# Forming the low halves of split weights with an accumulating transfer, in a conformer block

## The chip, the cores and the metric

The kernel runs on one core of one Trainium2 chip. A time is the device time of one execution in microseconds (us). The engines of the core are TensorE (PE, matrix products), VectorE (DVE), ScalarE (ACT), GpSimd (POOL) and SyncE (SP); each works through its own list of instructions in order, and they meet only at semaphores. SP issues nearly all transfers between DRAM and on-chip memory; here a few will be issued by POOL.

## The reference

The block takes a sequence of 1024 tokens with 1024 channels, in float32:

```
h = rms_norm(x, norm1_g)
z = h @ w_in                       # 1024 x (2*1024 + 3*1024 + 2*1024) columns
glu, q, k, v, gates = split(z)
a = value(glu) * sigmoid(gate(glu))          # the gated unit
a = silu(rms_norm(causal_conv31(a)));  y_a = a @ w_conv_out
q, k = rms_norm per head of 64;  o = dilated attention over three groups, 16 heads
y_b = o @ w_attn_out
x = x + (g_a * y_a + g_b * y_b) @ w_out
x = x + gated feed-forward with a convolution of width 3 (2816 wide)
```

Only the projection of `h` onto the columns of the gated unit and of q, k and v is touched by the change.

## The kernel before

**Split products.** A float32 product is made of three faster ones. Each operand is split into a high half, the value rounded to the shorter format (float32r) that TensorE takes, and a low half, the rest. The product is high x high + high x low + low x high. The function `split` (L74) does it: ACT copies the source into the high half (L76), DVE subtracts the high half from the source (L77).

**Weights.** A piece of weights is 128 x 1024 floats, 512 KB. `stage` (L79) has SP load it into a `raw` buffer, and `wsplit` (L84) makes `hi` and `lo` from it. There are four buffers each for `raw`, `hi` (tag `whi`) and `lo` (tag `wlo`), and all weights of the phase use them in turn. A new piece can be split only after the matmuls that read the piece four before it.

**The first phase.** `x` is normalised and transposed into `hT`, split too. Then come:

- the gated unit: for each of 8 channel blocks `c`, a product with a gate piece `g{c}` and one with a value piece `v{c}` (`gemm_ch`, 48 matmuls each), a sigmoid (ACT, L234) and a multiplication (DVE, L237) into `apad`;
- q, k, v: six chunks `ch` (q, k, v, twice), each with four pieces `qkv{ch}_0` to `qkv{ch}_3`. `gemm_tok` (L118) makes one block of 128 tokens by 24 matmuls: for each of 8 steps `k`, high x high (L125), high x low of the weights (L126), low x high (L127); piece `j` serves the steps 2j and 2j+1. Eight token blocks make a chunk, in four PSUM banks. `qkv_head` squares (ACT, L276), sums (DVE, L277), has POOL raise to the power -0.5 (L101) and scales (DVE, L280); `qkv_tail` transposes the result (PE, L288), splits it and stores it in DRAM. The tail lags two token blocks behind;
- the gates (`gate_steps`), and the depthwise convolution of width 31 (`conv_branch`), which is all on DVE: 8 blocks of 31 passes over 128 x 1024 floats (L250, L253).

After that the heads of the attention start (`head`, `score`), in memory that the first phase gives back when the convolution is through.

**The order.** The kernel is written in one order, and a planner sets the order on each engine: it simulates the whole program with its own durations and gives each engine, at each moment, the first written instruction that is ready in the simulation. So DVE works on the convolution, written after q, k, v, in the gaps of the gated unit and of q, k, v. The matmuls of two token blocks can also be interleaved where a piece is late in the simulation. On the chip the order is fixed; every engine waits in place.

Of the kernel before, what the change touches and what calls it, by code (L numbers as in the profile page):

```python
# [12 lines left out]
F32 = mybir.dt.float32  # L13
F32R = mybir.dt.float32r
AF = mybir.ActivationFunctionType
ALU = mybir.AluOpType
# [4 lines left out]
P = 128  # L21
# [29 lines left out]
def block_kernel(ctx: ExitStack, tc: tile.TileContext, x, g1, g2, pack, mask,  # L51
                 w_ch, w_qkv, w_co, w_ao, w_o, w_up, w_down, out):
    nc = tc.nc
    act, dve, pool, pe, sp = nc.scalar, nc.vector, nc.gpsimd, nc.tensor, nc.sync

    cst = ctx.enter_context(tc.tile_pool(name="cst", bufs=1))
    wp = ctx.enter_context(tc.tile_pool(name="wp", bufs=1))
# [4 lines left out]
    def big_ps(name):  # L62
        return psA.tile([P, T], F32, tag="A", name=name)

    def bank_ps(name):
        return psB.tile([P, 512], F32, tag="B", name=name)
# [12 lines left out]
    def stage(src, name):  # L79
        raw = wp.tile([P, 1024], F32, tag="raw", bufs=4, name=f"raw_{name}")  # L80
        sp.dma_start(raw.rearrange("p (a b) -> p a b", a=src.shape[1]) if len(src.shape) == 3 else raw, src)
        return raw

    def wsplit(src, name):  # L84
        hi = wp.tile([P, 1024], F32R, tag="whi", bufs=4, name=f"hi_{name}")[:, : src.shape[1]]
        lo = wp.tile([P, 1024], F32R, tag="wlo", bufs=4, name=f"lo_{name}")[:, : src.shape[1]]
        split(hi, lo, src)
        return hi, lo

    def wpiece(src, name):  # L90
        raw = stage(src, name)
        hi, lo = wsplit(raw, name)
        if len(src.shape) == 3:
            hi = hi.rearrange("p (a b) -> p a b", a=src.shape[1])
            lo = lo.rearrange("p (a b) -> p a b", a=src.shape[1])
        return hi, lo

    def rstd_of(dst, ssq, n, tmp):
# [4 lines left out]
    def gemm_half(o, w, actT, half):  # L103

        hi, lo = w
        ah, al = actT[0][half], actT[1][half]
        for k in range(KT):
            pe.matmul(o, hi[:, k, :], ah[:, k, :], start=(k == 0), stop=False)  # L108
            pe.matmul(o, hi[:, k, :], al[:, k, :], start=False, stop=False)  # L109
            pe.matmul(o, lo[:, k, :], ah[:, k, :], start=False, stop=(k == KT - 1))  # L110
            yield

    def gemm_ch(ps, w, actT):
        for half in range(2):
            for _ in gemm_half(ps[:, half * 512 : half * 512 + 512], w, actT, half):
                pass

    def gemm_tok(ps, actT, wpieces, tt):  # L118

        half, c0 = tt // 4, (tt % 4) * P  # L120
        for k in range(KT):
            hi, lo = wpieces[k // 2]
            ah = actT[0][half][:, k, c0 : c0 + P]
            al = actT[1][half][:, k, c0 : c0 + P]
            pe.matmul(ps, ah, hi[:, k % 2, :], start=(k == 0), stop=False)  # L125
            pe.matmul(ps, ah, lo[:, k % 2, :], start=False, stop=False)  # L126
            pe.matmul(ps, al, hi[:, k % 2, :], start=False, stop=(k == KT - 1))  # L127
# [50 lines left out]
    def hb_tiles(pl, name):  # L178
        t = [[pl.tile([P, KT, 512], F32R, tag=f"hb{a}{h}", name=f"{name}{a}{h}") for a in range(2)]
             for h in range(2)]  # L180
        return [[t[h][a] for h in range(2)] for a in range(2)]
# [15 lines left out]
    with tc.tile_pool(name="ph1", bufs=1) as p1:  # L197
# [4 lines left out]
        for tt in range(8):  # L202
            xx = p1.tile([P, CW - 1 + T], F32, tag="apad", bufs=10, name=f"x_{tt}")[:, 0:T]
            sp.dma_start(xx, x[tt * P : (tt + 1) * P, :])
            xt.append(xx)
            if tt == 3:
                wfirst = [wpiece(w_ch[8], "g0"), wpiece(w_ch[0], "v0")]
# [7 lines left out]
        hT = hb_tiles(hb1, "hT")  # L215
# [12 lines left out]
        for c in range(8):  # L228
            a = p1.tile([P, CW - 1 + T], F32, tag="apad", bufs=10, name=f"apad_{c}")
            pool.memset(a[:, : CW - 1], 0.0)  # L230
            gp = big_ps(f"glug_{c}")
            gemm_ch(gp, wfirst[0] if c == 0 else wpiece(w_ch[8 + c], f"g{c}"), hT)
            sg = t4(f"sg_{c}")
            act.activation(sg, gp, AF.Sigmoid)  # L234
            vp = big_ps(f"gluv_{c}")
            gemm_ch(vp, wfirst[1] if c == 0 else wpiece(w_ch[c], f"v{c}"), hT)
            dve.tensor_tensor(out=a[:, CW - 1 :], in0=vp, in1=sg, op=ALU.mult)  # L237
            apad.append(a)

# [25 lines left out]
        def qkv_head(ch, tt, ps):  # L265
            kind, g8 = ch % 3, ch // 3
            psv = ps.rearrange("p (h d) -> p h d", h=8)
            if kind == 2:
                vt = t4(f"v_{ch}_{tt}", F32R).rearrange("p (h s d) -> p h s d", h=8, s=2)
                split(vt[:, :, 0, :], vt[:, :, 1, :], psv)  # L270
                spill(dv[g8][:, :, tt, :], vt.rearrange("p h s d -> p h (s d)"))
                return None
            sq = p1.tile([P, 512], F32, tag="sq", bufs=2, name=f"sq_{ch}_{tt}")
            ss = p1.tile([P, 8], F32, tag="ss8", bufs=2, name=f"ss8_{ch}_{tt}")
            rs = p1.tile([P, 8], F32, tag="rs8", bufs=2, name=f"rs8_{ch}_{tt}")
            act.activation(sq, ps, AF.Square)  # L276
            dve.tensor_reduce(out=ss, in_=sq.rearrange("p (h d) -> p h d", h=8), axis=AX.X, op=ALU.add)  # L277
            rstd_of(rs, ss, DH, ss)
            qn = p1.tile([P, 512], F32, tag="qn", bufs=3, name=f"qn_{ch}_{tt}")
            dve.tensor_tensor(out=qn.rearrange("p (h d) -> p h d", h=8), in0=psv,  # L280
                              in1=rs.unsqueeze(2).to_broadcast([P, 8, DH]), op=ALU.mult)
            return ch, tt, qn

        def qkv_tail(ch, tt, qn):
            kind, g8 = ch % 3, ch // 3
            pt = big_ps(f"qt_{ch}_{tt}")[:, 0:512]
            for j in range(4):
                pe.transpose(pt[:, j * P : (j + 1) * P], qn[:, j * P : (j + 1) * P], ident)  # L288
            qh = p1.tile([P, 512], F32R, tag="qh", bufs=2, name=f"qh_{ch}_{tt}")
            ql = p1.tile([P, 512], F32R, tag="ql", bufs=2, name=f"ql_{ch}_{tt}")  # L290
            if kind == 0:
                act.activation(qh, pt, AF.Copy, scale=qkg)
                dve.scalar_tensor_tensor(out=ql, in0=pt, scalar=qkg, in1=qh.bitcast(F32),
                                         op0=ALU.mult, op1=ALU.subtract)
            else:
                split(qh, ql, pt)
            dst = dq if kind == 0 else dk
            for s, t in ((0, qh), (1, ql)):
                spill(dst[g8][s][:, :, tt * P : (tt + 1) * P], t.rearrange("p (a b) -> p a b", a=4))

        tails = []
        for ch in range(6):
            kind, g8 = ch % 3, ch // 3
            wpieces = [wpiece(w_qkv[kind * 2 + g8, :, 2 * j : 2 * j + 2, :], f"qkv{ch}_{j}") for j in range(4)]
            for tt in range(8):
                ps = bank_ps(f"qkv_{ch}_{tt}")
                gemm_tok(ps, hT, wpieces, tt)
                tails.append(qkv_head(ch, tt, ps))
                if len(tails) > LAG:
                    t = tails.pop(0)  # L310
                    if t is not None:
                        qkv_tail(*t)
# [161 lines left out]
    with tc.tile_pool(name="ph3", bufs=1) as p3:  # L474
# [48 lines left out]
        for j in range(2):  # L523
            wpieces = [wpiece(w_o[j, :, 2 * i : 2 * i + 2, :], f"wo{j}_{i}") for i in range(4)]
# [32 lines left out]
        def up_first(f):  # L557

            v = stage(w_up[f], f"uv{f}")
            vh, vl = wsplit(v, f"uv{f}")  # L560
            xz = big_ps(f"xz_{f}")
            product(xz[:, 0:512], four(vh)[:, 0:4], four(vl)[:, 0:4], *left[0], True)
            product(xz[:, 512:1024], four(vh)[:, 4:8], four(vl)[:, 4:8], *left[1], True)
            return v, xz
# [46 lines left out]
    with tc.tile_pool(name="ph4", bufs=1) as p4:  # L611
# [43 lines left out]
        for f in range(FT):  # L655
            up_rest(f, *ready.pop(0))
            if f + 1 < FT:
                v, xz = ups.pop(0) if ups else up_first(f + 1)
# [6 lines left out]
    with tc.tile_pool(name="ph5", bufs=1) as p5_:  # L665
# [7 lines left out]
        def gload(k, half, fs, dst=None):  # L673
            raw = dst if dst is not None else p5_.tile([P, G * 512], F32, tag="gr", bufs=4, name=f"gr{k}{half}_{fs[0]}")
            for i, f in enumerate(fs):
                sp.dma_start(raw[:, i * 512 : i * 512 + 512], dff[k * HF + f][:, half * 512 : half * 512 + 512])
            return raw[:, : len(fs) * 512]
# [41 lines left out]
        for fs in groups:  # L719
            e = early.pop(0) if early else None  # L720
            g = gload(0, 0, fs, dst=None if e is None else e[:, 0].bitcast(F32))
# [137 lines left out]
```

## Time and profile before

| | us |
|---|---|
| median of 3 runs (1814.44 to 1816.28) | 1815.06 |
| the profiled execution | 1811.43 |
| its span, first to last instruction | 1809.6 |
| PE busy | 1765.8 |
| DVE busy | 1318.8 |
| ACT busy | 771.6 |
| POOL busy | 195.8 |

The mean clock granted to TensorE is 0.991 of full speed. "Busy" is time with an instruction running; matmuls overlap, so a matmul row of 390 ns in the profile stands for one every 0.227 us when they follow each other. Rows of the timeline give the start, the duration, the engine, the line, the operation, what it writes and reads, and in brackets how long its engine sat idle just before it and what ended that. A row of windows gives busy time (and number of instructions) per engine, the granted clock, the busy share of the DMA engines and the rate.

### The profile page before, as it was taken

To read this page: it belongs to the slowest core of one execution; us is meant where nothing else is said; L and a number is where in the kernel's file an instruction comes from. 1 tells how busy PE (TensorE), PEld (TensorE's weight loads), DVE (VectorE), ACT (ScalarE), POOL (GpSimd) and SP (SyncE) were. 2 spreads that over 40 slices of the span, in tenths; PEclk is the share of its full clock that TensorE was granted. 3 is DMA by queue.
4 is the path that set the end of the run, shared out by engine and by line. 5 is a ranking of instruction groups with operands and counts; after the bars stand their busy time and mean duration, and the time that the engine had idled before them with its cause. 6 is when DMAs were issued, how large, how long until landed. Compare 5 with 4: busy or idle time off the path is not lost.

```text
span 1809.6 us, 22474 instructions
## 1 busy us (share of the span) xinstructions
PE 1765.8 (98%) x8244; PEld 1461.9 (81%) x8244; DVE 1318.8 (73%) x1798; ACT 771.6 (43%) x1202; POOL 195.8 (11%) x197
## 2 busy tenths in 40 slices
PE   7999999999999999999999999989999999999999
PEld 5888888888887888887888878768888888878887
DVE  5999999999735655666654543787777777789863
ACT  4111132232245656666655332545444554543441
POOL 1000133133002122222210000210000000000000
PEclk9999999999999999999999999999999999999999
DMA  5111145345549456666527543313222222389851
GB/s 203 59 47 47 41 134 163 116 134 157 157 173 246 145 158 175 180 165 179 164 70 279 169 160 133 104 48 107 80 82 81 71 95 91 116 303 335 298 180 47
DMA packets 142063, 257.57 MB, mean 142 GB/s; under 512 B 11265, under 2 KB 60545, under 8 KB 141953
## 3 DMA queue, kind: packets, MB, share of 16 engines
q1 hardware_dynamic: 141808, 255.61, 43.8%
q8 instruction: 65, 1.06, 0.3%
q10 hardware_dynamic: 144, 0.52, 0.1%
q14 instruction: 46, 0.37, 0.1%
HBM read 190.03 MB, written 66.06 MB: 142 GB/s over the span
## 4 chain that ended last, share of the span: by engine, by line
PE 53%; DMA 4%; DVE 4%; issue 1%; ACT 1%; SPq 1%; POOLq 0%; POOL 0%; DVEq 0%; ACTq 0%
PE xz L550 5%; PE xz L551 5%; PE xz L552 5%; PE dx L703 5%; PE dy L703 5%; DMA gg<-dya 2%; PE pp L400 2%; PE y L550 2%; PE y L552 2%; PE y L551 2%; PE ya L108 2%; PE ya L109 2%; PE ya L110 2%; PE o L408 2%; PE wo L126 1%; PE wo L127 1%
## 5 line engine op out<-in xcount | busy, mean ns | idle before, releaser
L253 DVE SCALAR_TENSOR_TENSOR cacc<-apad,pk,cacc 128x1024 f32<-128x1024 f32 x240 | 297.7, 1274 | 0.7
L125 PE MATMUL qkv<-hi_qkv,hT 128*128 128x512 f32 x384 | 151.8, 396 | 0.0
L127 PE MATMUL qkv<-hi_qkv,hT 128*128 128x512 f32 x384 | 150.0, 391 | 0.0
L126 PE MATMUL qkv<-lo_qkv,hT 128*128 128x512 f32 x384 | 149.4, 390 | 0.0
L389 DVE CUSTOM_DVE_ANT_0 p<-s,m 128x128 f32<-128x128 f32 (+7 forms) x128 | 95.1, 750 | 62.7 <-PE pp L400 39.0
L77 DVE TENSOR_TENSOR pl<-pp,ph 128x512 fp32r<-128x512 f32 x192 | 103.1, 549 | 49.1 <-ACT ph L76 48.6
L393 POOL TENSOR_SCALAR p<-p,st 128x128 f32<-128x128 f32 (+7 forms) x128 | 94.9, 748 | 335.5 <-DVE st L392 211.9
L76 ACT ACTIVATE ph<-pp 128x512 fp32r<-128x512 f32 x192 | 91.3, 487 | 92.2 <-PE pp L400 89.3
L649 DVE SCALAR_TENSOR_TENSOR u<-u,pk 128x1023 f32<-128x1023 f32 (+1 forms) x88 | 112.3, 1279 | 18.9 <-ACT u L647 18.5
L101 POOL TENSOR_TENSOR rs<-ss,mhalf 128x8 f32<-128x8 f32 (+1 forms) x40 | 80.3, 2010 | 353.1 <-DVE ss L100 353.0
L391 ACT ACTIVATE p<-p,st 128x128 f32<-128x128 f32 (+7 forms) x128 | 99.0, 776 | 14.6 <-DVE st L389 12.9
L108 PE MATMUL gate<-hT,hi_gt 128*128 128x512 f32 x256 | 101.8, 398 | 0.0
L109 PE MATMUL gate<-hT,hi_gt 128*128 128x512 f32 x256 | 100.8, 394 | 0.0
L110 PE MATMUL gate<-hT,lo_gt 128*128 128x512 f32 x256 | 100.3, 393 | 0.0
L400 PE MATMUL pp<-ident,p 128*128 128x128 f32 x576 | 94.4, 277 | 0.0
L127 PEld LDWEIGHTS qkv<-hi_qkv,hT 128*128 128x128 f32 x384 | 72.0, 188 | 15.3
L126 PEld LDWEIGHTS qkv<-lo_qkv,hT 128*128 128x128 f32 x384 | 72.2, 188 | 14.5 <-DVE lo_qkv L77 0.3
L125 PEld LDWEIGHTS qkv<-hi_qkv,hT 128*128 128x128 f32 x384 | 72.2, 188 | 14.0
L400 PEld LDWEIGHTS pp<-ident,p 128*128 128x128 f32 x576 | 69.5, 142 | 10.0 <-issue 0.2
L384 PE MATMUL s<-kh,q 128*128 128x512 f32 (+1 forms) x192 | 69.7, 368 | 7.3 <-DVE st L389 4.8
L408 PE MATMUL o<-ph,v 128*128 128x512 f32 x192 | 73.1, 381 | 3.6 <-ACT ph L76 1.8
L409 PE MATMUL o<-pl,v 128*128 128x512 f32 x192 | 70.5, 369 | 1.6 <-DVE pl L77 1.5
(269 smaller groups left out, 4610.4 us busy)
## 6 DMA issues: line engine op xcount, KB each, us to landing
wr<-w_down SPq DMA_DIRECT2D x45, 512.0 KB, 5.7
gr<-dff SPq DMA_DIRECT2D x62, 256.0 KB, 5.2
raw_qkv<-w_qkv SPq DMA_DIRECT2D x24, 512.0 KB, 3.9
raw_uv<-w_up SPq DMA_DIRECT2D x22, 512.0 KB, 3.3
raw_ug<-w_up SPq DMA_DIRECT2D x22, 512.0 KB, 3.3
dff<-u SPq DMA_DIRECT2D x22, 512.0 KB, 2.6
dv<-v SPq DMA_DIRECT2D x16, 512.0 KB, 3.2
raw_gt<-w_ch SPq DMA_DIRECT2D x16, 512.0 KB, 4.8
```

The lines of the kernel that those rows point to most:

```text
L108: pe.matmul(o, hi[:, k, :], ah[:, k, :], start=(k == 0), stop=False)
L109: pe.matmul(o, hi[:, k, :], al[:, k, :], start=False, stop=False)
L110: pe.matmul(o, lo[:, k, :], ah[:, k, :], start=False, stop=(k == KT - 1))
L125: pe.matmul(ps, ah, hi[:, k % 2, :], start=(k == 0), stop=False)
L126: pe.matmul(ps, ah, lo[:, k % 2, :], start=False, stop=False)
L127: pe.matmul(ps, al, hi[:, k % 2, :], start=False, stop=(k == KT - 1))
L253: dve.scalar_tensor_tensor(out=acc, in0=a[:, j : j + T], scalar=w(j), in1=acc, op0=ALU.mult, op1=ALU.add)
L400: pe.transpose(pp[:, qb * P : (qb + 1) * P], pts[qb][:, kt * P : (kt + 1) * P], ident)
L550: pe.matmul(o, wh[:, k, :], bh[:, k, :], start=(start and k == 0), stop=False, skip_group_check=not start)
L551: pe.matmul(o, wh[:, k, :], bl[:, k, :], start=False, stop=False, skip_group_check=not start)
L552: pe.matmul(o, wl[:, k, :], bh[:, k, :], start=False, stop=(k == 3), skip_group_check=not start)
L703: pe.matmul(banks[n], a[:, c], b[:, d], start=(start and i == 0 and m == 0), stop=(stop and i == nf - 1 and m == 2), skip_group_check=True)
```

## The change

A second way to form a piece, `wpiece_sum`, serves the weights of the gated unit (all but the first two pieces, so 14) and of q, k, v (all 24). The raw piece is still loaded by SP and ACT still copies it into the high half. ACT then writes the negated high half into the `lo` buffer, and a transfer issued by POOL adds the raw weights to it, read a second time from DRAM. DVE's subtraction is gone for these 38 pieces. The other weights (gates and all later phases) keep `wpiece`.

```diff
+    def wpiece_sum(src, name):
+
+        raw = stage(src, name)
+        hi = wp.tile([P, 1024], F32R, tag="whi", bufs=4, name=f"hi_{name}")
+        lo = wp.tile([P, 1024], F32R, tag="wlo", bufs=4, name=f"lo_{name}")
+        act.activation(hi, raw, AF.Copy)
+        act.activation(lo, hi.bitcast(F32), AF.Copy, scale=-1.0)
+        hi = hi.rearrange("p (a b) -> p a b", a=src.shape[1])
+        lo = lo.rearrange("p (a b) -> p a b", a=src.shape[1])
+        pool.dma_start(lo, src, accum_op=ALU.add)
+        return hi, lo
...
-            gemm_ch(gp, wfirst[0] if c == 0 else wpiece(w_ch[8 + c], f"g{c}"), hT)
+            gemm_ch(gp, wfirst[0] if c == 0 else wpiece_sum(w_ch[8 + c], f"g{c}"), hT)
...
-            gemm_ch(vp, wfirst[1] if c == 0 else wpiece(w_ch[c], f"v{c}"), hT)
+            gemm_ch(vp, wfirst[1] if c == 0 else wpiece_sum(w_ch[c], f"v{c}"), hT)
...
-            wpieces = [wpiece(w_qkv[kind * 2 + g8, :, 2 * j : 2 * j + 2, :], f"qkv{ch}_{j}") for j in range(4)]
+            wpieces = [wpiece_sum(w_qkv[kind * 2 + g8, :, 2 * j : 2 * j + 2, :], f"qkv{ch}_{j}") for j in range(4)]
```

## The prediction

> **What bounds the kernel now.** I read the page's busy times first, then the windows of the first phase, then who TensorE waits for. From the page:
>
> ```profile
> PE 1765.8 (98%) x8244; PEld 1461.9 (81%) x8244; DVE 1318.8 (73%) x1798; ACT 771.6 (43%) x1202; POOL 195.8 (11%) x197
> PE   7999999999999999999999999989999999999999
> DVE  5999999999735655666654543787777777789863
> ```
>
> DVE looks full for the first quarter, but so does PE, and the windows say which of them matters (columns: PE, PE weight loads, DVE, ACT, POOL, granted clock, DMA share, GB/s):
>
> ```profile
> 45.00:100.00 55.00, 54.86 (x242) 45.12 (x241) 50.97 (x43) 10.15 (x10) 0.00 (x0) 1.00 0.17 58
> 200.00:250.00 50.00, 50.00 (x234) 41.38 (x233) 48.23 (x57) 14.74 (x20) 14.03 (x7) 1.00 0.22 66
> 400.00:450.00 50.00, 50.00 (x238) 41.33 (x237) 50.00 (x64) 13.25 (x21) 20.24 (x8) 1.00 0.49 146
> 500.00:520.00 20.00, 19.69 (x94) 16.25 (x93) 5.91 (x11) 3.96 (x5) 0.00 (x0) 1.00 0.27 93
> ```
>
> From 45 to 500 us PE is without a gap at full clock, although DVE is at 96 to 100% too. The list of TensorE's waits in the first 420 us confirms it: all of them are in the start-up.
>
> ```profile
> PE tp L190 <- DVE ss L100: 10.7, 2, 9.4
> PE tp L190 <- DVE xs L223: 1.9, 1, 1.9
> PE glug L108 <- ACT hT L76: 0.5, 1, 0.5
> ```
>
> So in this stage PE sets the time and DVE's load is cover: the convolution fills what is left of DVE, and is through just as the gates run. What DVE saves is worth nothing here; what delays a piece of weights is paid in full.
>
> **What is removed from DVE.**
>
> ```profile
> L77 DVE TENSOR_TENSOR lo_qkv<-raw_qkv,hi_qkv x24: 1203/1214/1226, 169.1 to 437.1; 128x1024 fp32r<-128x1024 f32 x24
> L77 DVE TENSOR_TENSOR lo_v<-raw_v,hi_v x8: 1215/1218/1220, 18.1 to 159.8; 128x1024 fp32r<-128x1024 f32 x8
> L76 ACT ACTIVATE hi_qkv<-raw_qkv x24: 1051/1062/1067, 168.0 to 432.6; 128x1024 fp32r<-128x1024 f32 x24
> ```
>
> 24 subtractions of 1.214 us and 14 of 1.218 are 46 us of DVE. They end up as an earlier convolution. Behind it, the nearest places where that could reach PE are the waits as attention opens, below the 500 us mark:
>
> ```profile
> PE s L384 <- DMA kl<-dk: 2.2, 1, 2.2
> 549.60:552.00 2.40, 1.53 (x4) 1.00 (x4) 0.09 (x1) 0.00 (x0) 0.00 (x0) 0.50 0.98 345
> 554.00:556.00 2.00, 1.90 (x6) 1.58 (x6) 1.29 (x8) 2.00 (x8) 0.90 (x3) 0.50 1.05 215
> ```
>
> The first head is loaded into memory that the convolution gives back. An earlier end could remove the 2.2 us, and 6.4 us at half clock behind it (549.6 to 556), worth 3.2. Bounds 0 and -5.4 us; I take -3.
>
> **What is added to ACT and the transfers.** 38 more copies of 1.06 us, 40 us on an engine busy 10 to 15 us of each 50: nothing, as long as no piece is waited for. 38 transfers of 512 KB, 19.9 MB over 450 us, are 44 GB/s on a stage that moves 58 to 146: nothing in sum; in bursts they count, below. `raw` is free after the high copy instead of after DVE, so the loads of raw weights only start earlier.
>
> **The gated unit.**
>
> ```profile
> 102.72 1.06 ACT L76 ACTIVATE hi_g<-raw_g 128x1024 fp32r<-128x1024 f32 x1 [9.82 <-PE glug L109]
> 113.60 1.06 ACT L76 ACTIVATE hi_v<-raw_v 128x1024 fp32r<-128x1024 f32 x1 [8.90 <-PE gluv L109]
> ```
>
> A buffer is freed at the end of a product, every 10.9 us, and its new piece is used three products later: 32.6 us of slack. The longer way of a piece (some 9 us, next part) lies inside it. Cost 0, with 23 us of cover left. The sigmoid queues behind one more ACT copy, 1 us, which nothing but DVE awaits.
>
> **The chunks of q, k, v.** Here the slack is short, since all four buffers hold the chunk in work. The end of chunk 0:
>
> ```profile
> 242.21 1.06 ACT L76 ACTIVATE hi_qkv<-raw_qkv 128x1024 fp32r<-128x1024 f32 x1 [0.76 <-PE qkv L127]
> 243.31 1.23 DVE L77 TENSOR_TENSOR lo_qkv<-raw_qkv,hi_qkv 128x1024 fp32r<-128x1024 f32 x1 [0.16 <-ACT hi_qkv L76]
> 243.57 1.06 ACT L76 ACTIVATE hi_qkv<-raw_qkv 128x1024 fp32r<-128x1024 f32 x1 [0.30 <-PE qkv L127]
> 246.45 0.48 PE L125 MATMUL qkv<-hi_qkv,hT 128*128 128x512 f32 x1
> 246.77 0.40 PE L126 MATMUL qkv<-lo_qkv,hT 128*128 128x512 f32 x1
> ```
>
> The last token block frees piece 0 at 241.9, and piece 1 1.36 us later (6 matmuls of 0.227). PE has 18 matmuls and a group of transposes left, and reads the new low half at 246.77. DVE had it ready at 244.54: 2.2 us to spare. The changed piece goes: high copy at 242.21, two copies of 1.06, done at 244.33. Then POOL issues and the transfer runs. The trace has no accumulating transfer and none issued by POOL, so I bound both. What rows there are, with the median time from issue to landing:
>
> ```profile
> raw_g<-w_ch SPq DMA_DIRECT2D x8, 512.0 KB, 3.3
> raw_qkv<-w_qkv SPq DMA_DIRECT2D x24, 512.0 KB, 3.9
> dq<-qh SPq DMA_DIRECT2D x16, 256.0 KB, 2.5
> x<-x SPq DMA_DIRECT2D x8, 512.0 KB, 8.4
> L81 SPq DMA_DIRECT2D raw_qkv<-w_qkv x24: 327/333/578, 126.9 to 391.7; - x24
> 239.65 2.54 POOL L101 TENSOR_TENSOR rs<-ss,mhalf 128x8 f32<-128x8 f32 x1 [3.10 <-DVE ss L100]
> ```
>
> Transfer: 256 KB more cost 3.3 - 2.5 = 0.8 us. Adding means reading the target too, which is one 512 KB more than the plain load: 3.9 + 1.6 = 5.5 us, nearest to the `raw_qkv` row. Bounds 3.3 (a plain quiet load) and 8.4 (the loads of x, in a queue full of them). Issue on POOL: between 0.33 us (SP's) and 2.54 (POOL's longest instruction here, behind which it may also have to queue); I take 1.0. The low half lands at 244.33 + 1.0 + 5.5 = 250.8, which is 4.1 us after PE wants it. By the low ends 1.2 us late, by the high ends 8.5.
>
> The Trainium skill, "DMA: Bandwidth & Descriptors", section "Specifications", gives first-byte latencies of about 1 us for transfers issued by GpSimd and 0.6 for those of SP. That speaks against the change: by it each landing is 0.4 us later and the sum 2 us larger. No row here shows it.
>
> The other three pieces come behind: ACT makes one per 2.12 us, and each transfer moves twice 512 KB, about 3 us at the 350 GB/s that windows here reach (345 in the row at 549.6). PE, if it interleaves two token blocks, uses a piece for 12 matmuls, 2.7 us. That it does so is shown by two squares close together at the head of the first chunk:
>
> ```profile
> 211.07 0.60 ACT L276 ACTIVATE sq<-qkv 128x512 f32<-128x512 f32 x1 [9.32 <-PE qkv L127]
> 212.20 0.60 ACT L276 ACTIVATE sq<-qkv 128x512 f32<-128x512 f32 x1 [0.53 <-PE qkv L127]
> ```
>
> So they trail by another 0.3 us each, 0.9 in all: 5.0 us of standing PE per transition. There is no other work for PE in that place: the gates need the same four buffers, and the tails bring only transposes. The first chunk is different, since only its fourth piece comes late (copied at 200.69, landing 209.3 by the same sum). Two blocks on three pieces cover 36 matmuls, until 208.9: cost about 0. That leaves 5 transitions, the first with its high copy at 242.21, the last here:
>
> ```profile
> 428.07 1.06 ACT L76 ACTIVATE hi_qkv<-raw_qkv 128x1024 fp32r<-128x1024 f32 x1 [0.76 <-PE qkv L127]
> ```
>
> **The clock behind a stall.** The one long wait of PE in mid-kernel is followed by half clock:
>
> ```profile
> PE y L551 <- DVE blk_t L77: 4.7, 1, 4.7
> PE wo L126 <- DVE lo_wo L77: 1.7, 1, 1.7
> 1180.00:1184.00 4.00, 4.00 (x10) 3.17 (x11) 4.00 (x6) 1.06 (x1) 1.76 (x1) 0.50 0.39 131
> 1060.00:1080.00 20.00, 17.18 (x75) 13.68 (x74) 11.60 (x16) 6.39 (x11) 0.00 (x0) 1.00 0.61 200
> ```
>
> After 4.7 us the clock is 0.50 for 4 us, a loss of 2 us; after 1.7 us it stays at 1.00; after the 2.2 us at `kl` it also fell. A stall of 5 us therefore costs 7. The Trainium skill, "TensorE: Matmul & The Clock Gate", Part 1, has the clock halve after an idle window of about 3.4 us. The trace disagrees at the 2.2 us wait, and the measurement decides. By the page, stalls of 2.2 to 3.4 us would go free of the 2 us, at most 10 us off the sum; with mine, nothing changes.
>
> **POOL's own queue.** Each of the 24 transfers is issued from the list that also holds the powers of L101. A transfer waiting for ACT's copy holds up the power behind it, then DVE's scaling and the transposes of the tail. The tail lags two blocks, 48 matmuls or 10.9 us, and POOL is busy 14 to 20 us of 50; 8 more in 48 us fit. Cost 0, inside the high end above if the cover fails.
>
> **The sum.** Against the profiled execution: 1811.4 + 5 x (5.0 + 2.0) - 3 = 1843.4 us. The median of the runs is 3.6 above that execution, so 1815.06 + 32 = 1847 us.
>
> **The rivals.** (a) *The transfers are slow or queue up.* The four pieces of a transition and the four raw loads for the chunk after it go out within some 10 us. With landings of 8.4 us and 5 us between pieces, the first is 244.33 + 1.0 + 8.4 - 246.77 = 7.0 us late and PE stands 7.0 + 3 x (5 - 2.7) = 14 us, with the clock 16; five of them 80, less 3: 1892 us. For it: the loads of x filled the DMA engines just so (share 1.03); against it: 0.22 to 0.49 in the windows above.
>
> ```profile
> 10.00:20.00 10.00, 6.36 (x31) 4.98 (x29) 9.32 (x14) 9.43 (x18) 1.56 (x6) 0.85 1.03 419
> ```
>
> (b) *The transfers are hidden.* With low ends for issue and landing a piece is 1.2 us late. If the planner puts the high x high matmuls of three more blocks first (0.7 us), PE stands 0.5 us and keeps its clock: 5 x 0.5 - 3, within 1 us of no change, 1814.5 us. Against it: it needs both low ends, and the planner's foresight.
>
> (c) *The early convolution wins.* The place is the opening of attention at 547 us, the price the 5.4 us above. It decides once a transition costs below 0.4 us, that is, with a landing up to 4.0 us after ACT's second copy (2.4 of slack, 0.7 of matmuls put first, 0.4, and some transposes). Then the time is 1815 - 5.4 + 1 = 1811 us. For it: DVE is at 96 to 100% until 489; against it: attention's other waits are for transfers and scores, not for the convolution.
>
> **How the numbers follow.** My forecast 0.62: 1847 us, its own range 1825 (transitions of 2 to 3 us, clock kept) to 1880 (13 each). (a) 0.20, (b) 0.09, (c) 0.09. A change below 0.2%, 3.6 us, can't be told from none here. (c) is faster and a part of (b) falls either way: faster 0.09, same 0.08, slower 0.83. The range goes from 1818, where (b) ends, to 1905, the middle of (a) and something above.
>
> **What would show it.** Right: PE waits at L126 on the landing of `lo_qkv` at five places some 47 us apart, 4 to 6 us each; half clock behind each; no waits in the gated unit; DVE's L77 without `lo_qkv`, and its idle time up in the first 500 us. Wrong: no waits at the chunk heads (b), waits at every piece (a), waits in the gated unit or of the transposes on POOL's powers (a queue that I priced at nothing), or a landing outside 3.3 to 8.4 us.

## The result, and the profile after

The changed kernel takes 1863.08 us (median of 4 runs, 1859.55 to 1864.13) against 1814.75 for the kernel before beside it: a ratio of 1.0268, 95% interval 1.0255 to 1.0281, or 48 us more. Forecast were 32 us more, 1847, with a range of 1818 to 1905. The direction, the place and the clock's part were right; one duration was too short, two parts had been priced at nothing, and one as a gain.

The page after, its busy times and the first slices:

```profile
span 1862.0 us, 22573 instructions
PE 1785.6 (96%) x8244; PEld 1475.3 (79%) x8244; DVE 1277.8 (69%) x1760; ACT 808.2 (43%) x1240; POOL 222.3 (12%) x235
PE   7999988889899999999999999989999999999999
DVE  4999988986124556666564542588777777779963
```

DVE has lost 41 us of work, and the span has grown by 52.4. PE, which had 9s from the second slice on, has 8s from the sixth: q, k, v. The windows that answer to those before (same columns):

```profile
45.00:100.00 55.00, 54.91 (x243) 45.15 (x242) 48.83 (x41) 16.44 (x16) 5.69 (x6) 1.00 0.53 115
200.00:250.00 50.00, 48.43 (x226) 39.89 (x224) 49.05 (x57) 15.69 (x21) 18.23 (x10) 1.00 0.32 79
250.00:300.00 50.00, 44.83 (x199) 36.71 (x200) 43.38 (x54) 11.55 (x19) 17.78 (x10) 0.93 0.54 148
400.00:450.00 50.00, 44.17 (x197) 36.16 (x197) 40.99 (x51) 17.00 (x23) 16.42 (x11) 0.93 0.61 158
```

The gated unit (45 to 200 us) runs as before, PE without a gap: 154.91 us busy of these 155, before 154.86. From 250 us on, 5 to 6 us of each 50 are idle and the granted clock is 0.93. Who TensorE waits for, in the whole run:

```profile
PE qkv L138 <- DMA lo_qkv<-w_qkv: 28.2, 5, 6.1
PE qt L300 <- DVE qn L292: 4.5, 2, 3.5
PE s L396 <- DMA kl<-dk: 1.8, 1, 1.8
```

Five waits on the landing of a low half, 5.6 us each, were not there before, and neither were two on the scaled heads of q and k (`qn`), which PE transposes into `qt`. The transfers themselves (the last figure is the median time to landing, which counts from the start of the issue), their issue on POOL, and the queue that they go through (packets, MB, share of the 16 DMA engines' time):

```profile
lo_qkv<-w_qkv POOLq DMA_DIRECT2D x24, 512.0 KB, 9.4
L107 POOL DMA_DIRECT2D lo_qkv<-w_qkv x24: 865/876/1392, 172.0 to 478.4; - x24
q0 software_dynamic: 5472, 19.93, 6.1%
```

And the head of the second chunk, where the prediction had worked its sum:

```profile
243.04 1.06 ACT L103 ACTIVATE hi_qkv<-raw_qkv 128x1024 fp32r<-128x1024 f32 x1 [0.76 <-PE qkv L139]
244.13 1.06 ACT L104 ACTIVATE lo_qkv<-hi_qkv 128x1024 fp32r<-128x1024 f32 x1
245.50 0.93 POOL L107 DMA_DIRECT2D lo_qkv<-w_qkv  x1 [1.84 <-ACT lo_qkv L104]
247.94 0.48 PE L137 MATMUL qkv<-hi_qkv,hT 128*128 128x512 f32 x1
254.16 0.76 PE L138 MATMUL qkv<-lo_qkv,hT 128*128 128x512 f32 x1 [5.74 <-DMA lo_qkv<-w_qkv]
256.43 0.63 PE L137 MATMUL qkv<-hi_qkv,hT 128*128 128x512 f32 x1
258.53 0.40 PE L139 MATMUL qkv<-hi_qkv,hT 128*128 128x512 f32 x1
```

The copies end at 245.19, POOL issues at 245.50, and PE goes on at 254.16, 8.7 us after the issue. It would have gone on at 248.17, one matmul (0.227 us) after the last one on the high half, so 6.0 us are lost, and the matmuls take 0.63 us instead of 0.40 until 258: half clock. The windows there show where the landing falls. The DMA engines are full:

```profile
248.00:252.00 4.00, 0.43 (x3) 0.11 (x1) 4.00 (x6) 4.00 (x7) 1.65 (x2) 0.96 0.97 196
252.00:256.00 4.00, 1.84 (x4) 1.49 (x5) 4.00 (x6) 1.46 (x2) 3.11 (x3) 0.50 1.04 296
260.00:264.00 4.00, 4.00 (x21) 3.28 (x20) 0.37 (x1) 0.00 (x0) 0.00 (x0) 1.00 1.04 223
```

**Where the 52.4 us of the span come from.** Up to the last matmul of q, k, v it is 47.4 (the last starts at 524.6 instead of 477.2). 28.2 are the waits on landings, 4.5 those on the heads. Six of these seven are followed by half clock, 7 to 13 matmuls at 0.427 instead of 0.227 us, 1.6 to 2.9 us each: 13. The first matmul of q, k, v comes 0.8 later. That is 46.5 of the 47.4. Behind q, k, v are 5 us more. 2.9 of them lie in the product with w_out, where the clock is half for 3.4 us (window clock 0.83) behind a wait that both kernels have; the run with the transfer in the gated unit alone, which is as fast as the kernel before, shows the same 0.83. So I do not put them down to the change. The other 2.1 lie in attention, in small waits.

### The profile page after: what moved, and what is told of

The parts are those of the page before. It is cut to its first block, busy times and chain, and to the rows that moved or that the text cites. A ratio compares the mean times of both kernels' runs of the same rounds, so it can differ in the third digit from the quotient of the medians.

```text
span 1862.0 us, 22573 instructions
## 1 busy us (share of the span) xinstructions
PE 1785.6 (96%) x8244; PEld 1475.3 (79%) x8244; DVE 1277.8 (69%) x1760; ACT 808.2 (43%) x1240; POOL 222.3 (12%) x235
## 4 chain that ended last, share of the span: by engine, by line
PE 52%; DMA 4%; DVE 4%; ACT 1%; issue 1%; SPq 0%; POOL 0%; DVEq 0%; ACTq 0%; POOLq 0%
PE xz L562 5%; PE xz L563 5%; PE xz L564 5%; PE dx L715 5%; PE dy L715 5%; PE pp L412 2%; PE y L562 2%; PE y L563 2%; PE y L564 2%; PE ya L120 2%; PE ya L121 2%; PE ya L122 2%; PE o L420 2%; PE wo L138 2%; PE wo L139 1%; PE wo L137 1%
## 5 line engine op out<-in xcount | busy, mean ns | idle before, releaser
L138 PE MATMUL qkv<-lo_qkv,hT 128*128 128x512 f32 x384 | 155.9, 407 | 28.2 <-DMA lo_qkv<-w_qkv 28.2
L137 PE MATMUL qkv<-hi_qkv,hT 128*128 128x512 f32 x384 | 155.1, 407 | 0.0
L139 PE MATMUL qkv<-hi_qkv,hT 128*128 128x512 f32 x384 | 154.7, 403 | 0.0
L113 POOL TENSOR_TENSOR rs<-ss,mhalf 128x8 f32<-128x8 f32 (+1 forms) x40 | 73.9, 1850 | 132.0 <-DVE ss L112 131.9
L139 PEld LDWEIGHTS qkv<-hi_qkv,hT 128*128 128x128 f32 x384 | 75.6, 197 | 15.9
L137 PEld LDWEIGHTS qkv<-hi_qkv,hT 128*128 128x128 f32 x384 | 75.1, 196 | 15.4
```

## The experiments

Times are medians; "before" is the kernel before, run beside them on the same chip. Each cut of code is against the changed kernel and shortened.

### Which pieces pay

The gated unit alone:

```diff
-wpieces = [wpiece_sum(w_qkv[kind * 2 + g8, ...
+wpieces = [wpiece(w_qkv[kind * 2 + g8, ...
```

> The accumulating transfer serves the gated unit alone; q, k and v keep the subtraction on DVE. Theory (only the chunk heads of q, k, v pay, because all four buffers are in use there and a low half lands some 8.6 us after its issue): within 3 us of the kernel before, no wait of PE on lo_g or lo_v, and none on lo_qkv. Rival 1 (the transfers, POOL's issues or the full DMA engines cost everywhere): 14 of 38 pieces, so about +18 us. Rival 2 (the relief of DVE, 17 us here, is worth something): 3 to 6 us faster than before.

1814.25 us, before 1814.95; ratio 0.9996 (0.9982 to 1.0009). No wait on any low half.

q, k, v alone:

```diff
-gemm_ch(gp, ... wpiece_sum(w_ch[8 + c], f"g{c}"), hT)
+gemm_ch(gp, ... wpiece(w_ch[8 + c], f"g{c}"), hT)
-gemm_ch(vp, ... wpiece_sum(w_ch[c], f"v{c}"), hT)
+gemm_ch(vp, ... wpiece(w_ch[c], f"v{c}"), hT)
```

> The accumulating transfer serves q, k and v alone; the gated unit keeps DVE's subtraction. Theory: as the changed kernel, +45 to +52 us over the kernel before, five waits of PE on lo_qkv of 5 to 6 us each, half clock behind each. Rival 1 (a cost per transfer wherever it is): 24 of 38, so about +31 us.

1858.52 us, 1.0241 (1.0222 to 1.0261): 43.6 us more than before, just under the band that I gave, and well above the 31 of a cost per transfer.

```profile
PE qkv L138 <- DMA lo_qkv<-w_qkv: 31.2, 5, 7.3
```

So the same transfer costs nothing in the gated unit, where 32.6 us of slack cover it, and in q, k, v it costs 43.6 of the 48.3 us, with intervals of the two ratios that overlap.

### What the relief of DVE is worth

```diff
-lo = wp.tile([P, 1024], F32R, tag="wlo", bufs=4, name=f"lo_{name}")
+lo = low0[0]            # written once
 act.activation(hi, raw, AF.Copy)
-act.activation(lo, hi.bitcast(F32), AF.Copy, scale=-1.0)
...
-pool.dma_start(lo, src, accum_op=ALU.add)
```

> The low halves of these 38 pieces are left out: no subtraction, no negated copy, no transfer; all of them read one buffer that is written once. It leaves out part of the computation and measures the relief of DVE (46 us) by itself, with nothing put in its place. Theory (PE sets the time here and the earlier convolution waits for TensorE's fixed order anyway): within 2 us of the kernel before. Rival (an earlier convolution opens attention earlier): 3 to 6 us faster, the wait on kl gone.

1817.97 us, before 1814.95; 1.0011 (0.9999 to 1.0023). With 38 subtractions taken away (46 us by their rows; DVE's busy time falls by 40) and nothing put in their place, nothing is gained. The last pass of the convolution starts at 443.1 instead of 484.8 us, but the first head is loaded no earlier, and its wait stays (first the kernel before, then this run):

```profile
L133 SPq DMA_DIRECT2D kl<-dk x32: 444/594/1199, 541.3 to 878.2; - x32
L143 SPq DMA_DIRECT2D kl<-dk x32: 444/593/1648, 541.2 to 879.7; - x32
PE s L396 <- DMA kl<-dk: 3.5, 1, 3.5
```

In the written order 92 steps of the gates stand between q, k, v and attention, and the multiplication of the convolution's result by its norm starts at 519.2 us here and at 519.3 before. That these steps are the reason is read from the order and was not tried by itself.

### What makes the landing long

The same transfer without the add:

```diff
-pool.dma_start(lo, src, accum_op=ALU.add)
+pool.dma_start(lo, src)
```

> The transfer that POOL issues copies the raw weights over the low buffer and adds nothing, so the low halves are wrong; everything else is as in the changed kernel. Theory (the add itself is dear: it keeps the DMA engines busy about 1.8 times as long as a plain load of the same size, 2.99 against 1.63 us per transfer by the queues' shares): median landing of lo_qkv falls from 9.4 to about 7 us, waits of PE on lo_qkv from 28 to 16 to 20 us, and the time is some 8 to 14 us below the changed kernel. Rival (the cost is POOL's software path, and the add is free): landing 9 us and the time as the changed kernel.

1853.24 us, 9.8 below the changed kernel. The landing falls from 9.4 to 7.0 us, as expected, and the waits from 28.2 to 22.2, less than the 16 to 20 expected:

```profile
lo_qkv<-w_qkv POOLq DMA_DIRECT2D x24, 512.0 KB, 7.0
q0 software_dynamic: 5472, 19.93, 3.4%
L107 POOL DMA_DIRECT2D lo_qkv<-w_qkv x24: 527/537/1027, 172.0 to 470.7; - x24
```

The share of the queue gives the engine time of one transfer: 6.1% of 1862.0 us over 38 is 2.99 us of all 16 engines with the add, 3.4% of 1848.9 over 38 is 1.65 without. The add nearly doubles it (1.8 times) and takes a third of a microsecond more to issue. The Trainium skill, "Collectives: The Full Stack", section "The bandwidth ceiling: the fold count and why AG ≠ RS ≠ AR", has the reducing step of a collective at half the rate of the copying one, because it reads two sources. The transfer here is no collective; its shares come near that, at 1.8.

The adds alone, without the raw loads for the chunks 1 to 5:

```diff
+if ch == 0:
+    raws0 = [stage(w_qkv[0, :, 2 * j : 2 * j + 2, :], f"raw0_{j}") for j in range(4)]
-wpieces = [wpiece_sum(w_qkv[...], f"qkv{ch}_{j}") for j in range(4)]
+wpieces = [wpiece_sum(w_qkv[...], f"qkv{ch}_{j}", raws0[j]) for j in range(4)]
```

> The loads of raw weights for the chunks 1 to 5 of q, k, v are left out: their high halves are made from chunk 0's raw pieces, so they are wrong, and nothing but the accumulating transfers and the spills is moved at a chunk head. Theory (adds and raw loads share DMA engines that are full for some 18 us at each chunk head): the raw loads are 4 x 1.63 of some 22 us of engine time, so the median landing of lo_qkv falls from 9.4 to 6 or 7 us, waits of PE on lo_qkv from 28 to 13 to 20 us, time 8 to 16 us below the changed kernel. Rival (the add's own latency is 8.6 us there and the loads do not matter): landing and time as in the changed kernel.

1844.66 us, 18.4 below the changed kernel, somewhat more than the 8 to 16 expected; landing 6.6 us.

```profile
PE qkv L138 <- DMA lo_qkv<-w_qkv: 19.7, 6, 4.8
lo_qkv<-w_qkv POOLq DMA_DIRECT2D x24, 512.0 KB, 6.6
```

The add with its weights from the chip:

```diff
-pool.dma_start(lo, src, accum_op=ALU.add)
+pool.dma_start(lo, raw.rearrange("p (a b) -> p a b", a=src.shape[1]).bitcast(F32), accum_op=ALU.add)
```

> The accumulating transfer reads the raw weights from their buffer on the chip instead of a second time from DRAM; raw buffers are held until it has landed. Theory (the engine time of the add, 2.99 us per transfer on all 16 engines, and the queue of other transfers at the chunk heads decide, not DRAM): median landing of lo_qkv 8 to 10 us, time within 8 us of the changed kernel. Rival (the second read from DRAM is the slow part): landing 2 us or more shorter and the time 10 us or more below the changed kernel.

1846.69 us, 16.4 below the changed kernel. My figures were missed and the rival's were met, the second read from DRAM as the slow part. But the run changes more than that read. The raw buffer stays in use until the add has landed, so the next chunk's raw loads are issued later. In the changed kernel the first of them is issued at 244.13, ahead of the first add; here it comes behind that add's landing, 4.5 us after the issue:

```profile
245.76 0.92 POOL L107 DMA_DIRECT2D lo_qkv<-raw_qkv  x1 [1.84 <-PE qkv L138]
250.28 0.33 SPq L81 DMA_DIRECT2D raw_qkv<-w_qkv  x1
lo_qkv<-raw_qkv POOLq DMA_DIRECT2D x24, 512.0 KB, 6.1
lo_g<-raw_g POOLq DMA_DIRECT2D x7, 512.0 KB, 4.4
q0 software_dynamic: 5472, 19.93, 5.6%
```

The engine time hardly falls (5.6% of 1845.4 over 38: 2.72 us), but the landing does: by 1.1 us for the gate pieces of the gated unit (5.5 from DRAM), by 3.3 in the median of q, k, v. What PE waits for is the first add of a chunk, and its landings at the five heads separate the parts better than the medians. In the changed kernel they are 7.4 to 8.5 us; without raw loads 5.7 to 7.1, near the 5.5 of the quiet; with the weights from the chip 4.5 to 4.8, near the quiet 4.4. So the larger part, some 2 us, goes with the raw loads, and the second read from DRAM takes 1.1 us in the quiet and 1.2 to 2.3 here; no run takes that read away and leaves the raw loads in their place. The reading that I had set against the rival, a queue of other transfers at the head, is not refuted by this run.

The gain is not all in the landing, either: the waits on landings fall from 28.2 to 11.9 us, and those at the transposes rise from 4.5 to 11.5.

### Whether it is the place: more slack, or fewer late pieces

Two more buffers, and the control with the same cuts and no new buffers:

```diff
-apad bufs=10, t4 bufs=4, sq bufs=2
+apad bufs=9, t4 bufs=2, sq bufs=1          # both runs
...
+hi = own.tile([P, 1024], F32R, tag="xhi", bufs=2, ...)   # piece 0 of a chunk, first run only
+lo = own.tile([P, 1024], F32R, tag="xlo", bufs=2, ...)
```

> The changed kernel with two more buffers: the first piece of each chunk of q, k, v has two of its own, so that the first two pieces of a chunk can be formed while the chunk before is still in work. To make room apad has 9 buffers instead of 10, t4 2 instead of 4, sq 1 instead of 2. Theory (the transfer is fine, its place at the head of a chunk with all buffers in use is the cost): waits of PE on lo_qkv below 8 us in all, time within 15 us of the kernel before, 35 us or more below the run with the same cuts and no new buffers. Rival (DMA time or POOL is the limit): no more than 10 us below that run.

> Control for the run with more buffers: the changed kernel with the same cuts (apad 9, t4 2, sq 1) and no new buffers. Both theories: as the changed kernel, 0 to 10 us more for the cuts.

1831.24 us with the buffers, 1866.62 without: 35 us. The landings are as long as ever, the waits are a third:

```profile
PE qkv L142 <- DMA lo_qkv<-w_qkv: 9.0, 3, 3.9
lo_qkv<-w_qkv POOLq DMA_DIRECT2D x24, 512.0 KB, 9.6
```

The theory's band was missed by a hair (9.0 us of waits where I gave 8, 17.7 us above before where I gave 15); its core, that the same transfers cost less where they have slack, is shown. The 17.7 us that stay are about what the run without any transfer, below, costs; 9.0 of them are still waits on landings, and the cuts alone cost 3.5, so the likeness proves nothing.

The first two pieces of each chunk back on DVE:

```diff
-wpieces = [wpiece_sum(w_qkv[...
+wpieces = [(wpiece if j < 2 else wpiece_sum)(w_qkv[...
```

> In each chunk of q, k, v the first two pieces go back to DVE's subtraction, the last two keep the accumulating transfer; the gated unit as in the changed kernel. Theory (the slack of a piece decides: the later pieces have more when PE interleaves token blocks, and half as many adds queue): waits of PE on lo_qkv 0 to 2 us per chunk, 0 to 20 us over the kernel before. Rival (each late piece costs its own 6 us): half of the added time stays, about +25 us.

1836.11 us, 22.6 above before. This is the rival's figure rather than mine. The waits on landings were 10.9 us in 5, about 2 us per chunk as the theory had it, but others came beside them:

```profile
PE qkv L138 <- DMA lo_qkv<-w_qkv: 10.9, 5, 3.8
PE qt L300 <- DVE qn L292: 5.7, 3, 3.2
PE qkv L138 <- DVE lo_qkv L77: 1.6, 1, 1.6
```

That a stall at a low half isn't the whole cost made me take the transfer away altogether.

### Without the transfer

```diff
-pool.dma_start(lo, src, accum_op=ALU.add)
+dve.tensor_tensor(out=lo, in0=raw, in1=lo.bitcast(F32), op=ALU.add)
```

> ACT still writes the negated high half into the low buffer, but DVE adds the raw weights, for all 38 pieces; no transfer by POOL. It keeps the longer way through ACT and undoes the transfer. Theory (the landing of the transfer is the cost; a piece with two ACT copies and one pass of DVE is ready about 1 us later than before, against 2.2 us of slack): within 5 us of the kernel before, waits of PE at the low halves of q, k, v below 4 us in all. Rival (the serial ACT copies, 2.1 us per piece against 1.36 us between the pieces freed, cost a good part): +10 us or more.

1832.38 us, 1.0101 (1.0080 to 1.0122): 18 us above before, with no transfer at all. My theory (within 5 us) fell, and the time is the rival's (+10 or more). What is left of the change is the second ACT copy, ahead of a DVE pass. Who TensorE waits for in this run, at q, k, v:

```profile
PE qt L300 <- DVE qn L292: 9.1, 3, 4.7
PE qkv L138 <- DVE lo_qkv L105: 3.4, 3, 2.2
```

The larger part is not at the low halves. The longest wait, on four engines:

```profile
412.12 0.60 ACT L288 ACTIVATE sq<-qkv 128x512 f32<-128x512 f32 x1 [4.80 <-PE qkv L139]
413.25 0.60 ACT L288 ACTIVATE sq<-qkv 128x512 f32<-128x512 f32 x1 [0.53 <-PE qkv L139]
414.56 1.26 DVE L289 TENSOR_REDUCE ss<-sq 128x8 f32<-128x512 f32 x2
415.75 2.46 DVE L265 SCALAR_TENSOR_TENSOR cacc<-apad,pk,cacc 128x1024 f32<-128x1024 f32 x2
418.80 0.22 DVE L112 TENSOR_SCALAR ss<-ss 128x8 f32<-128x8 f32 x2
419.09 6.61 POOL L113 TENSOR_TENSOR rs<-ss,mhalf 128x8 f32<-128x8 f32 x2 [9.01 <-DVE ss L112]
424.13 0.69 DVE L292 TENSOR_TENSOR qn<-qkv,rs 128x512 f32<-128x512 f32 x1 [1.53 <-POOL rs L113]
424.97 0.72 PE L300 MATMUL qt<-ident,qn 128*128 128x128 f32 x4 [4.72 <-DVE qn L292]
```

Two token blocks end 1.1 us apart. DVE sums both, and works at two passes of the convolution and one other instruction before it scales the sums, 3.0 us after; the powers then run behind each other on POOL, 6.61 us for the two, DVE scales, and PE has nothing before the transposes. ACT is not what is late: it was idle for 4.80 us before the first square and made no weight copy from 405 to 425 us. What differs is the order on PE: the first four squares of this chunk start within 8.2 us (412.12 to 420.29), and in the kernel before within 13.0 (395.55 to 408.55). I took it for the tails and let them lag by three blocks instead of two, in this kernel and in the changed one:

```diff
-if len(tails) > LAG:
+if len(tails) > 3:          # and qn with 4 buffers
```

> The kernel without the transfer (ACT's negated copy, DVE adds) with the tails of q, k, v lagging three token blocks instead of two, and a fourth qn buffer. It asks whether the 18 us of that kernel come from the tails: its PE waits 9.1 us for scaled heads (qn) and 3.4 us for low halves, because the planner interleaves three or four blocks at a chunk head, whose heads then all come at once. If so: waits of PE at qt fall below 3 us and the time by 6 to 14 us, to 1818 to 1826. Rival (the serial ACT copies hold up the low halves, and the tails only show it): the waits move from qt to lo_qkv and the time stays within 4 us of 1832.

> The changed kernel with the same longer lag. Its waits are 28.2 us on the transfers' landings and 4.5 us on qn. If the landings rule: at most 8 us faster than the changed kernel, the five waits on lo_qkv still there. Rival (the tails are the larger part, the landings only show them): 15 us or more faster.

1836.66 us (waits at qt 10.9 in 4) and 1865.84 us (waits on landings 30.1 in 5): no gain in either. The rival that had the waits move to the low halves isn't met either, they stayed at qt. The longer formation alone costs 18 us. Up to the end of q, k, v the profiled run is 20.7 us behind: 12.5 of seen waits, 5 at half clock behind the three waits at the transposes, 1.4 by which q, k, v start later. For the longest wait the rows above speak for the order that the planner writes around the longer chain, and against ACT's second copy on the chip. For the 3.4 us at the low halves and for the whole that is not settled: no run has the longer chain in the old order.

No run was faster than the kernel before by more than its interval.

## Why the prediction was right, and where it was off

- *PE sets the time, DVE is cover.* Right, and shown: without the 38 subtractions, and nothing in their place, the time is the same (1.0011, 0.9999 to 1.0023).
- *The gated unit, cost 0.* Right: 0.9996 (0.9982 to 1.0009).
- *The chunk heads, five transitions of 5.0 us.* Five waits came, of 5.6 us each. The mechanism was right, and terms in it were off in opposite senses, so that the 5.0 came so near is partly luck. From the end of ACT's copies to the landing I had put 1.0 us for the issue and 5.5 for the transfer, 6.5; at the first head PE went on after 9.0 (245.19 to 254.16), and the landings of the first pieces were 7.4 to 8.5, with the issue in them. (The landing rows count from the start of the issue, so my 1.0 stood in the sum twice.) The slack behind the copies was 3.0 instead of 2.4. The trailing of the later pieces, put at 0.9, was nothing: no piece but the first of a chunk was waited for. The 5.5 is what the quietest adds took (median 5.5 for `lo_g`, 6.7 for `lo_v`, both in the gated unit); what I had put aside was the crowd, four adds and the four raw loads for the chunk after, in the same ten microseconds. It stood in rival (a), whose 14 us per head did not come.
- *Issue on POOL, 1.0 us.* Measured 0.88.
- *Half clock, 2.0 us per stall.* Right: 1.6 to 2.9 us, 7 to 13 matmuls at 0.427 instead of 0.227.
- *The early convolution, -3 us.* Wrong: 0. The step that failed is that an earlier end of the convolution opens attention earlier: in the run without low halves it ended 42 us earlier, the first head was loaded at 541.2 us as before (541.3), and the wait on `kl` was still there.
- *POOL's queue and the tails, cost 0.* Wrong in size: 4.5 us of waits at the transposes and one half clock, 6.2 us. But they did not come in the way that I had feared, a power held up behind a transfer. Before the longer of the two, 3.54 us until 390.86, POOL had stood idle for 22.64 us (the row behind this list). The four token blocks before it end within 5.2 us of each other (squares at 382.15 to 387.36; before the change 9.1, 351.99 to 361.05), so here too the blocks come close together and PE has nothing before the transposes.
- *ACT's second copy, nothing.* Wrong as a step. Without any transfer the longer way through ACT still costs 18 us. I had looked at how busy ACT is, and at the 2.2 us of slack of the first piece, and not at what a later low half does to the order around it. These 18 us are not a part of the 48 to be taken off: in the changed kernel the waits at the transposes are 4.5 us, in that run 9.1.

The powers ahead of the longer wait at the transposes, in the changed kernel:

```profile
386.69 5.02 POOL L113 TENSOR_TENSOR rs<-ss,mhalf 128x8 f32<-128x8 f32 x2 [22.64 <-DVE ss L112]
```

The sum, 32 us against 48.3 measured, lacks 3 (five heads at 5.6), 1.4 (the half clock behind them, 11.4 instead of 10), 3 (the convolution) and 6.2 (the tails), 14 of the 16. The rest is no larger than the 4 us by which the distance of the two profiled runs, 52.7, exceeds that of the medians; the 0.8 at the start of q, k, v and the 5 us behind q, k, v, which the runs do not tie to the change, are of that size.

## What to carry to other kernels

Before work is moved off a busy engine, ask whether that engine ends the wait of the one that sets the time; here it never did, and its relief was worth nothing. A transfer in place of a pass over the chip's memory is free where its result is wanted 30 us later and dear where all buffers are in use and the next user stands 5 us behind the freed one; price it by the landing in that place, with everything that is released there at the same moment, and not by the quiet one. Where a planner orders the engines, a longer chain can change the order as well, so a part priced at nothing deserves a run of its own. And a run that moves a transfer's source may move other transfers too, as the one with the weights from the chip did: look at when they are issued before its result is put down to the source.

## What the runs showed of the hardware

An accumulating transfer of 512 KB issued by POOL took 0.88 us to issue and 2.99 us of all 16 DMA engines, a plain one from the same queue 0.54 and 1.65; in the gated unit the gate pieces landed after 5.5 and 3.7 us (medians, from the start of the issue), the value pieces after 6.7 and 4.9, and with the added data on the chip both after 4.4.

The clock can fall after PE has started again. In the run without raw loads:

```profile
353.67 0.47 PE L138 MATMUL qkv<-lo_qkv,hT 128*128 128x512 f32 x1 [3.83 <-DMA lo_qkv<-w_qkv]
354.21 0.40 PE L137 MATMUL qkv<-hi_qkv,hT 128*128 128x512 f32 x1
354.81 0.63 PE L139 MATMUL qkv<-hi_qkv,hT 128*128 128x512 f32 x1
357.80 0.45 PE L137 MATMUL qkv<-hi_qkv,hT 128*128 128x512 f32 x1
```

The first matmuls behind the 3.83 us wait run at full rate, those from 354.4 to 357.8 at half. The Trainium skill, "TensorE: Matmul & The Clock Gate", Part 1, lets the clock fall after an idle window of about 3.4 us. In these runs it fell behind waits of 3.0 and 3.5 us, behind one of 2.2 before the change, and not behind one of 3.3 (until 379.46 us in the run with the weights from the chip, granted clock 1.00 after it); the measured waits do not give a fixed limit.
